# A linear-attention kernel: the store before the last is issued in five parts

## The chip, the cores and the metric

The kernel runs on one core of a Trainium2 chip. The metric is device time in microseconds (us) of one execution; smaller is better. Before the change three runs took 123.59 to 123.68 us, with a median of 123.68.

A core has five engines with instruction queues of their own: PE (matmul; its weight loads are listed as PEld), DVE (vector), ACT (scalar), POOL (general) and SP (which only synchronizes and issues transfers here). Transfers between the chip's main memory and the on-chip memory of 128 partitions are done by 16 DMA engines, and are issued from POOL, SP or ACT.

## The reference

Inputs Q, K and V are float32 of shape 8 x 12 x 512 x 64 (batch, heads, sequence, feature). For each of the 96 heads:

```
Q_feat = max(0, Q);  K_feat = max(0, K)
KV = K_feat^T V                      (64 x 64)
K_sum = sum of K_feat over the sequence
out = (Q_feat KV) / (Q_feat . K_sum + 1e-10)
```

The output has the shape of Q, in float32.

## The kernel before

The 96 heads are taken eight at a time, so there are NO = 12 groups, o = 0 to 11. One group of one tensor is 1 MB in main memory, seen as 128 partitions of 2048 float32, that is 8 KB in one run for each partition. A group of eight heads of output is such a block too.

Group 0 of K and V is loaded by SP and ACT as float32 into buffers that the output uses later (`k8`, `v8`). All other loads are issued by POOL (`load`, line 110), which converts to bf16 on the way: 4 KB a partition land in rings of six groups. The group's work runs through all engines: DVE masks and rectifies K and scales V (`prep`), PE transposes Q and multiplies K by V (`into`), ACT rectifies the transposed Q and copies KV, PE multiplies Q by KV and by K_sum, ACT copies the product (`ot`), PE transposes it back (`back`), and DVE multiplies it with the reciprocal of the denominator into one of eleven float32 buffers `o_sb` (`norm`, line 276). The groups overlap; group o's `norm` is done after group o+1's first half. At the end of its two halves, `norm` raises the semaphore NRM1.

Stores: `store(eng, o)` (lines 122 to 125) lets an engine wait for NRM1 and then issues one transfer of all 128 partitions from `o_sb` to the output. Groups 0 to 9 are stored from POOL, in POOL's queue between the loads and behind them. Groups 10 and 11 (NO - 2 and NO - 1) are stored from SP (lines 141 and 142), which has nothing else to do after its first load. POOL's transfers appear as queue q0 of the DMA engines, SP's as q1. Each completed transfer adds 16 to its semaphore: for the two stores of SP this is LAST.

SP ends the kernel: it waits for PE's last product (line 326), for the stores of POOL that no buffer's reuse waited for (ALL, line 327), and for LAST to reach 32 (line 328), and then clears the semaphores.

Of the kernel before, what the change touches and what calls it, by code (L numbers as in the profile page):

```python
# [5 lines left out]
def kernel(  # L6
# [9 lines left out]
    P = 128  # L16
# [4 lines left out]
    NO = B * H // 8  # L21
    assert NO * 8 == B * H and R == 16
    RING = 6
    NOUT = 11
# [7 lines left out]
    PE, PL, VE, AC, SP = nc.tensor, nc.gpsimd, nc.vector, nc.scalar, nc.sync  # L32

    def view(X):
        return X.rearrange("b h s d -> (b h s d)").rearrange("(n p f) -> n p f", p=P, f=RQ * D)

    Qr, Kr, Vr, Or = view(Q), view(K), view(V), view(out)

    def sb(name, shape, dt):
        return nc.alloc_sbuf_tensor(name, shape, dt)[:]  # L40
# [3 lines left out]
    def sems(*names):  # L44
        new = [nc.alloc_semaphore(n) for n in names]
        handles.extend(new)
        return new
# [9 lines left out]
    o_sb = [sb(f"o_sb{i}", [P, RQ, D], fp32) for i in range(NOUT)]  # L57
# [27 lines left out]
    ALL, LAST = sems("all", "last")  # L85
    stored = [sems(f"st{o}")[0] if o + NOUT < NO else ALL if o < NO - 2 else LAST for o in range(NO)]

    def land(name):
        landed[name], = sems(name)
        return landed[name]  # L90
# [4 lines left out]
    for eng, to, X, c in ((SP, k8, Kr, "k0"), (AC, v8, Vr, "v0")):  # L95
        d = eng.dma_start(out=to.rearrange("p r d -> p (r d)"), in_=X[0]).then_inc(land(c), 16)
# [22 lines left out]
        for i in range(o, o + n):  # L119
            run_of[i] = o  # L120

    def store(eng, o):
        eng.wait_ge(NRM1, o + 2)
        kw = {"single_packet": True} if eng is PL else {}
        eng.dma_start(out=Or[o], in_=o_sb[(o + 2) % NOUT].rearrange("p r d -> p (r d)"), **kw).then_inc(stored[o], 16)  # L125

    PL.memset(ident, 0.0).then_inc(ID, 1)
    PL.wait_ge(ID, 1)
# [2 lines left out]
    o, done = 1, 0  # L131
    for n in RUNS:
        while done < o + n - 1 - RING - HEAD + 1:
            store(PL, done)
            done += 1
        load(o, n)
        o += n
    assert o == NO
    for i in range(done, NO - 2):
        store(PL, i)  # L140
    for i in range(NO - 2, NO):
        store(SP, i)

    seen = set()

# [179 lines left out]

    SP.wait_ge(CO1, NO + 1)
    SP.wait_ge(ALL, 16 * (NOUT - 2))
    SP.wait_ge(LAST, 32)
    used = sorted(s.num for s in handles)
    assert used == list(range(used[0], used[-1] + 1))  # L330
    SP.sem_clear(range(used[0], used[-1] + 1))
# [28 lines left out]
```

## Time and profile before

The profile is of one execution of 123.92 us, of which the span from the first to the last instruction is 122.6 us.

| engine | busy us | share of the span |
|---|---|---|
| PE | 88.0 | 72% |
| DVE | 87.8 | 72% |
| ACT | 79.4 | 65% |
| POOL | 26.7 | 22% |

| transfers | issued | KB each on chip | median us from issue to landing |
|---|---|---|---|
| output, from POOL | 10 | 1024 | 39.0 |
| output, from SP | 2 | 1024 | 9.0 |
| Q, from POOL | 12 | 512 | 35.4 |
| K, from POOL | 11 | 512 | 32.1 |
| V, from POOL | 11 | 512 | 34.0 |

No compute engine is busy for more than 72% of the span. The long times from issue to landing are times in a queue: POOL issues well ahead of what the DMA engines can move. While loads run, the rate of the DMA engines in the profile counts the 4 KB that land of each 8 KB that are read, so 214 GB/s stand there where stores run at 425.

SP issues the store of group 10 at 106.79 us and that of group 11 at 113.45 us. The last store of POOL is issued at 98.44 us.

### The profile page before, as it was taken

The numbers are of one execution on the slowest core, as the hardware profiler recorded it, in microseconds if no ns is written. First come the engines' busy times: TensorE is split into PE (matmuls) and PEld (weight loads), VectorE is DVE, ScalarE is ACT, GpSimd is POOL, SyncE is SP. The second block draws the span as 40 slices with busy tenths as digits, with TensorE's granted clock in tenths as the row PEclk, the third lists the DMA queues.
The fourth block names the chain that finished last, engine by engine and source line by source line (L and its number), as shares of the span: only waits on it lengthen the run. The fifth ranks groups of instructions, "written<-read, shape, count | busy, mean of one in ns | idle before, by whom it ended". The sixth has DMA issues, their size and how long they took to land.

```text
span 122.6 us, 3398 instructions
## 1 busy us (share of the span) xinstructions
PE 88.0 (72%) x1480; PEld 75.4 (61%) x1480; DVE 87.8 (72%) x163; ACT 79.4 (65%) x109; POOL 26.7 (22%) x50
## 2 busy tenths in 40 slices
PE   0000069998998989989898998989899199768100
PEld 0000069986895958879596886958688189657100
DVE  1904924599999899999999999899993980927000
ACT  0043034999988888898889988888998285530000
POOL 2899700043050602409300101010010010000000
PEclk9999999999999999999999999999999959977855
DMA  3999999999999999999999999999999999999994
GB/s 80 401 317 214 214 210 212 212 212 214 214 214 214 214 214 214 215 214 214 214 214 212 214 214 212 214 212 341 255 214 298 428 425 428 425 428 425 425 430 182
DMA packets 6917, 32.56 MB, mean 266 GB/s; under 512 B 768, under 2 KB 768, under 8 KB 5120
## 3 DMA queue, kind: packets, MB, share of 16 engines
q0 software_dynamic: 6336, 28.31, 92.8%
q1 hardware_dynamic: 432, 3.15, 6.4%
q10 hardware_dynamic: 144, 1.05, 2.2%
q14 instruction: 4, 0.03, 0.1%
q8 instruction: 1, 0.02, 0.1%
HBM read 37.75 MB, written 12.58 MB: 410 GB/s over the span
## 4 chain that ended last, share of the span: by engine, by line
DMA 39%; PE 31%; DVE 19%; issue 1%; POOL 1%; ACT 1%; DVEq 0%
DMA q_all<-in_Q_dram 31%; DVE o_sb L276 13%; PE ps_kv L176 11%; PE ps_o L157 9%; DMA o_sb<-in_K_dram 8%; PE ps_q L169 6%; PE ps_o L197 4%; DVE kf L251 3%; DVE vo L257 2%; DVE q_sb L263 1%; ACT ot L237 1%; POOL v_all L117 1%; POOL k_all L117 0%; DVE den L287 0%; PE ps_q L189 0%
## 5 line engine op out<-in xcount | busy, mean ns | idle before, releaser
L276 DVE TENSOR_TENSOR o_sb<-ps_o,rec 128x1024 f32<-128x1024 f32 x24 | 28.4, 1220 | 8.5 <-PE ps_o L157 8.5
L237 ACT COPY ot<-ps_o 128x1024 f32<-128x1024 f32 x24 | 24.2, 1013 | 7.6 <-PE ps_o L197 6.2
L157 PE MATMUL ps_o<-ident,ot 128*128 128x128 f32 x208 | 27.2, 287 | 1.1 <-ACT ot L237 1.1
L176 PE MATMUL ps_kv<-vo,kf 64*128 64x132 bf16 x768 | 27.4, 225 | 0.0
L223 ACT ACTIVATE qt_sb<-ps_q 128x1024 bf16<-128x1024 bf16 x24 | 23.4, 1030 | 6.1 <-PE ps_q L169 6.1
L169 PE MATMUL ps_q<-ident,q_sb 128*128 128x128 bf16 x192 | 14.4, 235 | 16.3 <-DVE q_sb L263 16.3
L157 PEld LDWEIGHTS ps_o<-ident,ot 128*128 128x128 f32 x208 | 24.0, 147 | 2.7 <-ACT ot L237 1.4
L176 PEld LDWEIGHTS ps_kv<-vo,kf 64*128 64x128 bf16 x768 | 23.8, 97 | 2.9 <-issue 0.4
L169 PEld LDWEIGHTS ps_q<-ident,q_sb 128*128 128x128 bf16 x192 | 12.4, 106 | 18.7 <-DVE q_sb L263 16.3
L197 PE MATMUL ps_o<-qt_sb,kvd 128*128 128x256 bf16 x104 | 16.0, 279 | 8.7 <-DVE o_sb L276 8.3
L251 DVE TENSOR_SCALAR kf<-k_all,mask_k 128x1024 bf16<-128x1024 bf16 x44 | 18.4, 461 | 5.2 <-PE ps_kv L176 4.0
L228 ACT CAST kvd<-ps_kv 64x260 bf16<-64x260 f32 x48 | 18.0, 375 | 6.3 <-PE ps_kv L176 5.9
L197 PEld LDWEIGHTS ps_o<-qt_sb,kvd 128*128 128x128 bf16 x104 | 8.3, 99 | 13.8 <-DVE o_sb L276 12.0
L257 DVE TENSOR_SCALAR vo<-v_all,mask_v 128x1024 bf16<-128x1024 bf16 x33 | 14.9, 481 | 0.3 <-DMA v_all<-in_V_dram 0.3
L117 POOL DMA_DIRECT2D k_all<-in_K_dram x11 | 6.5, 592 | 32.7 <-DVE vo L257 32.5
L125 POOL DMA_DIRECT2D out_dram<-o_sb x10 | 5.3, 533 | 36.9 <-DVE o_sb L276 36.9
L217 ACT ACTIVATE vo<-v_all,mask_v 128x1024 bf16<-128x1024 bf16 x11 | 12.7, 1153 | 0.3
L263 DVE COPY q_sb<-q_all 128x2048 bf16<-128x2048 bf16 x12 | 8.3, 690 | 1.9 <-DMA q_all<-in_Q_dram 1.9
L117 POOL DMA_DIRECT2D v_all<-in_V_dram x11 | 7.8, 708 | 0.0
L189 PE MATMUL ps_q<-kvd,qt_sb 128*128 128x16 bf16 x208 | 7.5, 180 | 0.0
L189 PEld LDWEIGHTS ps_q<-kvd,qt_sb 128*128 128x128 bf16 x208 | 7.3, 96 | 0.3
L117 POOL DMA_DIRECT2D q_all<-in_Q_dram x11 | 6.7, 610 | 0.0
(21 smaller groups left out, 27.0 us busy)
## 6 DMA issues: line engine op xcount, KB each, us to landing
out_dram<-o_sb POOLq DMA_DIRECT2D x10, 1024.0 KB, 39.0
q_all<-in_Q_dram POOLq DMA_DIRECT2D x12, 512.0 KB, 35.4
k_all<-in_K_dram POOLq DMA_DIRECT2D x11, 512.0 KB, 32.1
v_all<-in_V_dram POOLq DMA_DIRECT2D x11, 512.0 KB, 34.0
out_dram<-o_sb SPq DMA_DIRECT2D x2, 1024.0 KB, 9.0
o_sb<-in_V_dram ACTq DMA_DIRECT2D x1, 1024.0 KB, 9.4
o_sb<-in_K_dram SPq DMA_DIRECT2D x1, 1024.0 KB, 9.6
```

Of the source, the lines that this page charges most:

```text
L117: PL.dma_start(out=t[:, to:to + n], in_=X[o:o + n].rearrange("n p f -> p n f"), single_packet=True).then_inc(land(f"{c}{o}"), 16)
L157: t = PE.transpose(ps_o[j][:, P * v:P * v + P], ot[:, 8 * j + v].rearrange("p h c -> p (h c)"), ident32)
L169: t = PE.transpose(dst[:, u], q_sb[:, j * (U // 2) + u], ident)
L176: t = PE.matmul(ps_kv[:, half, 0:2 * (D + 2)].rearrange("p (t d) -> p t d", t=2), kf[g][rows, r].rearrange("p s d -> p (s d)"), vo[g][rows ...
L189: t = PE.matmul(ps_den[:, u], qt_sb[:, u], kvd[:, :, 0:2 * D1:2 * D1 - 1], start=True, stop=True, skip_group_check=True)
L197: t = PE.matmul(ps[:, h], kvd[:, 4 * j + h, 1:2 * D + 1], q[:, :, 4 * j + h, :], start=True, stop=True, skip_group_check=True)
L223: AC.activation(qt_sb[:, j * (U // 2):(j + 1) * (U // 2)], ps_q[j].bitcast(bf16).rearrange("p (u f) -> p u f", u=U // 2), Act.Relu)
L228: t = AC.copy(kvd[64 * c:64 * c + 64, s::2, c * D1:c * D1 + D1].rearrange("p (g t) d -> p g t d", t=2), ps_kv[64 * s:64 * s + 64, :, 0:2 * ...
L237: t = AC.copy(ot[:, :, 4 * j:4 * j + 4], ps_o[j].rearrange("p (h u c) -> p u h c", h=4, u=U))
L251: VE.tensor_scalar(kf[g][:, :, s, :], k_rows(o, g), scalar1=0.0, scalar2=mask_k[:, s:s + 1], op0=Alu.max, op1=Alu.mult)
L257: x = VE.tensor_scalar(vo[g][:, :, t, 2:D + 2], v_rows(o, g), scalar1=mask_v[:, t:t + 1], scalar2=None, op0=Alu.mult)
L276: VE.tensor_tensor(dst[:, rs], ps_o[j].rearrange("p (r d) -> p r d", d=D), rec[o % 2][:, rs].unsqueeze(2).to_broadcast([P, R, D]), op=Alu. ...
```

## The change

The store of group 10 is issued as five transfers, of 112, 5, 5, 5 and 1 partitions in this order, one after the other from SP, behind one wait. The last store stays whole. As every part adds 16 to LAST, the wait at the end goes to 16 x 6 = 96.

```diff
-    def store(eng, o):
+    def store(eng, o, parts=(P,)):
         eng.wait_ge(NRM1, o + 2)
         kw = {"single_packet": True} if eng is PL else {}
-        eng.dma_start(out=Or[o], in_=o_sb[(o + 2) % NOUT].rearrange("p r d -> p (r d)"), **kw).then_inc(stored[o], 16)
+        to = 0
+        for n in parts:
+            eng.dma_start(out=Or[o, to:to + n], in_=o_sb[(o + 2) % NOUT][to:to + n].rearrange("p r d -> p (r d)"),
+                          **kw).then_inc(stored[o], 16)
+            to += n
+        assert to == P
...
-    for i in range(NO - 2, NO):
-        store(SP, i)
+
+    PARTS = (112, 5, 5, 5, 1)
+    store(SP, NO - 2, PARTS)
+    store(SP, NO - 1)
...
-    SP.wait_ge(LAST, 32)
+    SP.wait_ge(LAST, 16 * (len(PARTS) + 1))
```

## The prediction

> **What bounds the kernel now.** I read the page's slices first, then the chain that ended last, then SP's waits, then the last 16 us cut into short windows.
>
> The page's slices show which resource is full. The row "DMA" is the busy share of the 16 DMA engines in tenths, 3.07 us to a slice.
>
> ```profile
> DMA  3999999999999999999999999999999999999994
> GB/s 80 401 317 214 214 210 212 212 212 214 214 214 214 214 214 214 215 214 214 214 214 212 214 214 212 214 212 341 255 214 298 428 425 428 425 428 425 425 430 182
> ```
>
> The engines stand at nine tenths or more from the second slice to the last but one, while the page's rows of all compute engines show 0 in the last two. The end is set by the DMA engines emptying their queues. In the chain that ended last, the compute part stops long before the span's end of 122.6:
>
> ```profile
> 112.20 1.24 DVE o_sb L276
> 113.44 0.05 issue
> 113.48 0.61 PE ps_o L197 x4
> ```
>
> The chain follows instructions and so runs out at 114.1; the 8.5 us behind it are transfers. SP's waits say so:
>
> ```profile
> SPq L125 <- DVE o_sb L276: 111.2, 2, 104.9
> SPq L328 <- DMA out_dram<-o_sb: 8.6, 1, 8.6
> ```
>
> SP waits 8.6 us at line 328 for the two stores that it issued itself. The wait ends at 122.4, and nothing but the clearing of the semaphores follows.
>
> The windows of the tail (columns: window, its length, busy us of PE, PEld, DVE, ACT and POOL, PE's granted clock, DMA share, GB/s) show how the 16 engines stop:
>
> ```profile
> 113.50:119.60 6.10, 0.59 (x4) 0.29 (x4) 0.00 (x0) 0.00 (x0) 0.00 (x0) 0.66 1.02 430
> ...
> 120.20:120.50 0.30, 0.00 (x0) 0.00 (x0) 0.00 (x0) 0.00 (x0) 0.00 (x0) 0.50 0.90 382
> 120.50:120.80 0.30, 0.00 (x0) 0.00 (x0) 0.00 (x0) 0.00 (x0) 0.00 (x0) 0.50 0.59 246
> 120.80:121.10 0.30, 0.00 (x0) 0.00 (x0) 0.00 (x0) 0.00 (x0) 0.00 (x0) 0.50 0.40 164
> 121.10:121.40 0.30, 0.00 (x0) 0.00 (x0) 0.00 (x0) 0.00 (x0) 0.00 (x0) 0.50 0.20 82
> 121.40:121.70 0.30, 0.00 (x0) 0.00 (x0) 0.00 (x0) 0.00 (x0) 0.00 (x0) 0.50 0.13 55
> 121.70:122.00 0.30, 0.00 (x0) 0.00 (x0) 0.00 (x0) 0.00 (x0) 0.00 (x0) 0.50 0.01 0
> ```
>
> From the first line comes the price of a row (one partition of a store, 8 KB): 430 GB/s over 16 engines is 26.9 GB/s each, and 8192 bytes at that are 0.305 us. The others are a staircase. GB/s by 0.30 us by one row of 8192 bytes gives the rows begun in each window: 14, 9, 6, 3, 2 and none. As a row lasts as long as a window, these are engines still at work. Ten of the 16 begin nothing after 120.8; three begin something after 121.1, two after 121.4. The two last end near 121.8 (share 0.01 of 16 engines for 0.30 us is 0.05 us), and the wait ends 0.6 us later. If all engines stopped together, the six late ones' 6 + 3 + 2 = 11 rows would be shared by 16, so about 0.7 row or 0.2 us after 120.9 instead of 0.9. Some 0.7 us of unevenness is there; the page doesn't number the engines, so which ones are late it doesn't say.
>
> **The change part by part.** *Rows moved.* Parts of 112, 5, 5, 5 and 1 partitions, if they land on the engines as the change's own words have it, give every engine 7 rows, the first five three or (four of them) two more: 10 or 11 where all had 8. Against before, the first engine gets +3 rows (+0.915 us), the next four +2 (+0.61), the other eleven -1 (-0.305); 3 + 8 = 11, nothing is lost. Every engine is busy from the issue at 106.79 to its own end (shares of 1.01 and 1.02 from 106.8 to 119.6), so a row moved shifts the engine's end by the whole row.
>
> If the late engines are among the eleven, their end goes from 121.8 to 121.5. The first five then come from the ten that begin nothing after 120.8. These end between about 120.5 and 121.1, the middle at 120.8, and with their rows four end at 121.1 to 121.7 and the first at 121.4 to 122.0. The new last end lies between 121.5 and 122.0, a change of -0.3 to +0.2. I take -0.28, near the full row: rows begun fall from 14 to 9 between 120.2 and 120.8, and of those 9 six belong to engines that go on, so most of the ten are done by 120.8; besides, the wait ends 0.6 us after the last row, which leaves the first five some margin if their completion is quicker than the two last engines'.
>
> [...]
>
> *Issues.* Four more on SP. The two of before took 332 and 343 ns (SP's issues on line 125), so 4 x 0.338 = 1.35 us. They follow the wait for NRM1 that ends at 106.79, so the fifth is out by 108.5. Behind them in SP's queue stands the last store, which waits for DVE until 113.45. Cover 6.66 us, needed 1.7: nothing. Without the cover it would cost 1.35 us. No other engine waits for SP, and the q1 queue still has rows of the 112 by then (a store of 8 rows an engine took 9.0 us from issue to landing), so the late issue starves no engine. Bounds 0 and +1.35; I take 0.
>
> *Completions.* Each transfer brings 16 small packets (48 issues, 768 packets under 512 B on the page), and their time lies inside the 430 GB/s above. The parts of 5, 5, 5 and 1 bring four more to the first engine and three to the next four. Bounds: nothing, and a row's time for each, 1.22 on the first engine; by the 430 GB/s, which already hold such packets, I take 0.
>
> *The semaphore.* LAST counts to 96 where it counted to 32: one wait as before, behind which nothing stands. Zero.
>
> *Reading by sevens.* A store of 112 rows isn't cut over the engines as one of 128 is. An engine's seven rows may lie in partitions that another engine reads at that moment for POOL's stores. No row shows a transfer of another cut. Bounds by rows: 0, or each of seven rows taking the time of two and as many of the engine's other rows held up by strangers: 14 x 0.305 = 4.3 us. Rows of all 48 transfers keep one rate; I take 0, and the upper end makes a rival.
>
> Sum: 123.92 for the profiled execution (span 122.6 and 1.3 around it), less 0.28: 123.64. It stands 0.24 above the runs' median of 123.68, so for the median I predict 123.40.
>
> **Rivals.** *Engines in one another's way* (slower). Place: the seven rows of each engine, from 108 to 113, beside POOL's stores in the other queue. If partitions share a way out of the memory that carries about one engine's 26.9 GB/s, two engines on one way take 0.61 us for a row. One doubled row on a late engine eats the gain, a second makes it slower. Half the bound above, 2.1, less 0.3, gives 125.5; the whole 127.7. For it: the engines have no slack (shares of 1.0 to 119.6), so each stall reaches the end; the parts of five read neighbouring partitions at once. Against it: two queues feed the engines from 108.8 on, and a stalled row might be overlapped by the next. I hold it next in likelihood to the forecast.
>
> [...]
>
> *A late engine among the first five.* 121.8 + 0.61 or + 0.915, so +0.6 to +0.9: 124.3 to 124.6. It is the two engines that begin rows after 121.4 that decide: a third, ending near 121.5, would come to 122.1 with two more rows, neither gain nor much loss. Drawn blindly, both of the two are among the eleven with 11 x 10 / (16 x 15) = 0.46. Nothing on the page numbers them, so the profile speaks neither for nor against beyond that draw; I go above it for the forecast, since two engines that stand apart from the rest of the staircase are likelier a trait of certain engines than a draw, and there are more numbers from the sixth up.
>
> [...]
>
> *The parts don't go where they should.* If small parts spread over all engines, each keeps 8 rows: 123.68 with nothing gained, 123.9 with some small packets.
>
> **How the numbers follow.** A measurement of this kernel can tell about 0.2% (0.25 us). The forecast has 0.42, of which 0.35 over 0.2% faster and 0.07 within it, since -0.28 lies next to the border; engines in one another's way 0.32, all slower; a late engine among the five 0.21, slower; the parts elsewhere 0.05, of which 0.03 within and 0.02 slower. Faster 0.35, same 0.07 + 0.03 = 0.10, slower 0.32 + 0.21 + 0.02 = 0.55. The likeliest case's own range is 123.25 to 123.65. The range for 8 in 10 runs from 123.1 to 126.4: beyond it lie somewhat under half of engines in one another's way (0.14) and a little below.
>
> **What would show it.** Right: SP has six issues of stores, five of them from 106.8 to 108.5; the compute lines to 114.1 are unmoved; the tail's windows keep 430 GB/s up to 119.6, the staircase is steeper and SP's wait at 328 is some 0.3 us shorter. Engines in one another's way: the GB/s between 109 and 118 fall below 420 with the DMA share still at 1. A late one among the five: full rate, but one or a few engines still begin rows after 121.9. The forecast is wrong if the wait at 328 ends at 122.4 or later.

## The result, and the profile after

The changed kernel takes 124.47 us (median of 4 runs, 124.28 to 124.53) against 123.68 of before (now four runs, 123.59 to 124.01). The ratio is 1.0056, 95% interval 1.0035 to 1.0078: 0.8 us slower, where 0.28 us less was forecast. A second measurement of the same kernel (below) gave 1.0090, interval 1.0059 to 1.0122. The profiled execution took 124.53 us with a span of 123.2, against 123.92 and 122.6.

The page's slices of after, the same two rows as shown of before:

```profile
DMA  4999999999999999999999999999999999999992
GB/s 88 404 309 215 214 211 213 214 213 213 213 213 213 215 213 214 214 213 214 211 214 215 214 214 213 217 211 376 222 214 339 428 428 420 426 426 420 410 426 109
```

The loads' part is the same up to the small changes of any two executions. The DMA engines are full to the last slice but one again. The chain that ended last stops where it did (114.0 against 114.1), so the compute part did not move:

```profile
112.12 1.24 DVE o_sb L283
113.40 0.61 PE ps_o L204 x4
```

SP's waits, with the final one now at line 335:

```profile
SPq L127 <- DVE o_sb L283: 109.1, 2, 104.9
SPq L335 <- DMA out_dram<-o_sb: 9.3, 1, 9.3
```

It is 9.3 us where it was 8.6, and ends at 122.8 (plus 0.18 of its own) instead of 122.4. The windows of the tail (window, length, busy us of PE, PEld, DVE, ACT and POOL, PE's clock, DMA share, GB/s):

```profile
113.50:119.60 6.10, 0.51 (x4) 0.21 (x3) 0.00 (x0) 0.00 (x0) 0.00 (x0) 0.64 1.02 419
120.20:120.50 0.30, 0.00 (x0) 0.00 (x0) 0.00 (x0) 0.00 (x0) 0.00 (x0) 0.50 0.59 246
120.50:120.80 0.30, 0.00 (x0) 0.00 (x0) 0.00 (x0) 0.00 (x0) 0.00 (x0) 0.50 0.33 137
120.80:121.10 0.30, 0.00 (x0) 0.00 (x0) 0.00 (x0) 0.00 (x0) 0.00 (x0) 0.50 0.39 164
121.10:121.40 0.30, 0.00 (x0) 0.00 (x0) 0.00 (x0) 0.00 (x0) 0.00 (x0) 0.50 0.39 164
121.40:121.70 0.30, 0.00 (x0) 0.00 (x0) 0.00 (x0) 0.00 (x0) 0.00 (x0) 0.50 0.26 109
121.70:122.00 0.30, 0.00 (x0) 0.00 (x0) 0.00 (x0) 0.00 (x0) 0.00 (x0) 0.50 0.26 109
122.00:122.30 0.30, 0.00 (x0) 0.00 (x0) 0.00 (x0) 0.00 (x0) 0.00 (x0) 0.50 0.20 82
122.30:122.70 0.40, 0.00 (x0) 0.00 (x0) 0.00 (x0) 0.00 (x0) 0.00 (x0) 0.50 0.01 0
```

Two things differ from before. The rate from 113.5 to 119.6 is 419 GB/s, not 430, with the share at 1.02 as it was: the engines are busy all the time and move less. And the staircase is longer. By GB/s times 0.30 us over 8192 bytes the rows begun are 9, 5, 6, 6, 4, 4, 3, 0, where before they were 14, 9, 6, 3, 2, 0 in the windows from 120.2 on. Most engines stop earlier than before, which is the row less that they have; but six engines begin a row in each of the windows from 120.8 to 121.4, which fits five engines with added rows and one other late one (the table below bears this out). Three begin a row after 122.0, where before nothing began after 121.7.

### The profile page after: what moved, and what is told of

The parts are those of the page before. It is cut to its first block, busy times and chain, and to the rows that moved or that the text cites. A ratio compares the mean times of both kernels' runs of the same rounds, so it can differ in the third digit from the quotient of the medians.

```text
span 123.2 us, 3402 instructions
## 1 busy us (share of the span) xinstructions
PE 87.8 (71%) x1480; PEld 75.2 (61%) x1480; DVE 87.8 (71%) x163; ACT 79.4 (64%) x109; POOL 26.7 (22%) x50
## 4 chain that ended last, share of the span: by engine, by line
DMA 39%; PE 30%; DVE 19%; issue 1%; POOL 1%; ACT 1%; DVEq 0%
DMA q_all<-in_Q_dram 31%; DVE o_sb L283 12%; PE ps_kv L183 11%; PE ps_o L164 9%; DMA o_sb<-in_K_dram 8%; PE ps_q L176 6%; PE ps_o L204 4%; DVE kf L258 3%; DVE vo L264 2%; DVE q_sb L270 1%; ACT ot L244 1%; POOL v_all L117 1%; POOL k_all L117 0%; DVE den L294 0%; PE ps_q L196 0%
```

## The experiments

Two theories were set against each other after this result. L: late engines are among the first five, and their extra rows make the end. W, later sharpened to N: the way in which the store is cut costs; N says that rows which several engines read at once from neighbouring partitions last longer. The first five are the engines that the change's parts of five use, and the first is the one of them that the part of one uses: in the change's trace the same five of 16 chains of packets (below) have one row of each part of five, and one of the five chains has a fourth small row. That parts of other sizes take these engines in one and the same order is the author's assumption. All runs were timed beside runs of the kernel before on the same chip. The ratio is an estimate of its own, not the quotient of the two medians; where the two give different microseconds, the text says which is meant.

| run | what SP issues in place of the whole store of group 10 | median us | before beside it | ratio, 95% interval |
|---|---|---|---|---|
| e1 | 112, 16 | 124.05 | 123.79 | 1.0021 (1.0002 to 1.0041) |
| e2 | whole, and two loads of 5 neighbouring partitions | 124.62 | 123.79 | 1.0057 (1.0036 to 1.0077) |
| e3 | whole, and two loads of 1 partition | 123.72 | 123.79 | 0.9994 (0.9980 to 1.0009) |
| e4 | 112, 8, 8 | 124.27 | 123.79 | 1.0045 (1.0022 to 1.0068) |
| e5 | 112, four times 4, neighbours | 125.11 | 123.76 | 1.0095 (1.0066 to 1.0125) |
| e6 | 112, four times 4, every fourth partition | 124.42 | 123.76 | 1.0057 (1.0040 to 1.0074) |
| e7 | whole, and two loads of 5 spread partitions | 124.36 | 123.76 | 1.0037 (1.0021 to 1.0053) |
| e8 | 112, 15, 1 | 124.30 | 123.76 | 1.0028 (1.0009 to 1.0048) |
| e9 | 112, 5, 5, 5, 1, the fives in steps of three | 124.41 | 124.02 | 1.0046 (1.0032 to 1.0060) |
| e10 | the change again: 112, 5, 5, 5, 1 | 124.97 | 124.02 | 1.0090 (1.0059 to 1.0122) |
| e11 | whole, and two loads of 2 spread partitions | 123.93 | 124.02 | 1.0004 (0.9984 to 1.0024) |
| e12 | whole, and two loads of 4 spread partitions | 124.13 | 124.02 | 1.0015 (1.0003 to 1.0027) |

### Rows added to the first engines, nothing else changed

e2 and e3 keep before's store whole and add transfers behind it that only cost time. The loads fill a part of `k_all` that nothing reads any more; n is 5 or 1:

```diff
+    for x in range(2):
+        SP.dma_start(out=k_all[0:n, 2 * x:2 * x + 2].rearrange("p n r d -> p (n r d)").bitcast(fp32),
+                     in_=Kr[0, 0:n]).then_inc(LAST, 16)
```

> Before's whole store, and behind it two loads of 5 partitions of 8 KB each into a part of k_all that is no longer read: added work of two rows for each of the first five engines, none taken away. Theory L: the first five hold the last engine or one close to it, so the end moves by most of two rows, +0.4 to +0.6: 124.1 to 124.3. If the first five were among those that end at 120.5 to 121.1, the end moves by 0 to +0.1: 123.7 to 123.8. Theory W gives the latter too.

> As the run with loads of 5 partitions, with loads of 1 partition: two rows for the first engine alone. Theory L with the first engine itself late: +0.4 to +0.6, 124.1 to 124.3; with the late ones second to fifth: 123.7 to 123.8. Theory T: each added transfer costs whatever its rows, +0.2 to +0.3 here and in the run with 5.

Two rows more on the first engine alone change nothing (0.9994). Two on each of the first five make it 0.7 us longer. The windows of the tail of e3, then of e2:

```profile
121.10:121.40 0.30, 0.00 (x0) 0.00 (x0) 0.00 (x0) 0.00 (x0) 0.00 (x0) 0.50 0.20 82
121.40:121.70 0.30, 0.00 (x0) 0.00 (x0) 0.00 (x0) 0.00 (x0) 0.00 (x0) 0.50 0.01 0
```

```profile
121.10:121.40 0.30, 0.00 (x0) 0.00 (x0) 0.00 (x0) 0.00 (x0) 0.00 (x0) 0.50 0.33 137
121.40:121.70 0.30, 0.00 (x0) 0.00 (x0) 0.00 (x0) 0.00 (x0) 0.00 (x0) 0.50 0.26 109
121.70:122.00 0.30, 0.00 (x0) 0.00 (x0) 0.00 (x0) 0.00 (x0) 0.00 (x0) 0.50 0.20 82
122.00:122.30 0.30, 0.00 (x0) 0.00 (x0) 0.00 (x0) 0.00 (x0) 0.00 (x0) 0.50 0.07 27
```

With the added rows on one engine the last row begins before 121.4 (three engines in 121.1 to 121.4, then none), no later than in before. With five engines it begins after 122.0. Both runs add two transfers, so transfers as such (theory T in the expectations) cost nothing that can be seen. The first engine has room for two rows; somewhere among the second to fifth is one that has none. That is theory L. The measured 0.7 us (by the ratio, interval 0.45 to 0.95) is a little more than the two rows' 0.61.

### Which of the first five

e7, e11 and e12 do the same with loads of 5, 2 and 4 rows that go to partitions 25 apart:

```diff
-        SP.dma_start(out=k_all[0:n, 2 * x:2 * x + 2].rearrange("p n r d -> p (n r d)").bitcast(fp32),
-                     in_=Kr[0, 0:n]).then_inc(LAST, 16)
+        SP.dma_start(out=k_all[0:25 * n:25, 2 * x:2 * x + 2].rearrange("p n r d -> p (n r d)").bitcast(fp32),
+                     in_=Kr[0, 0:25 * n:25]).then_inc(LAST, 16)
```

> Before's whole store and two loads of 5 partitions behind it, as in the earlier run, but to partitions 0, 25, 50, 75 and 100 instead of 0 to 4. Two rows more for the first five engines. Theory L+N: +0.2 to +0.4, 124.0 to 124.2, less than the +0.7 with neighbouring partitions. Theory L alone: +0.6 to +0.8 again.

> Before's whole store and two loads of 2 partitions (0 and 25): two rows more for the first two engines. If the late one of the first five is the second: +0.3 to +0.5, 124.1 to 124.3, like the spread loads of 5. If it is among the third to fifth: 123.7 to 123.9.

> Before's whole store and two loads of 4 partitions (0, 25, 50, 75): two rows more for the first four engines. Late one among the second to fourth: 124.1 to 124.3. If it is the fifth alone: 123.7 to 123.9.

Two engines: nothing (1.0004). Four: 0.19 us by the ratio (0.0015 of 124.02), interval just clear of none. Five: 0.46 us by the ratio. So the second engine has room like the first, the third or fourth is somewhat late, and the fifth more. The times in the expectations were counted from a before of 123.8, and before stood at 124.02 beside e11 and e12, so the differences count: one late engine among the second to fourth was to give +0.3 to +0.5, the fifth alone nothing. The 0.19 lies between, and more than one late engine fits better.

The packets themselves tell which engines are late. An engine's packets follow one another without a gap (in these traces the next begins 3 ns before the end of the last), so the packets of a trace sort into 16 chains. The number of 8 KB rows that a chain has between two completions of SP's queue shows whether its engine took part in a small transfer. The last packet of a chain ends at, in us:

| run | engines with added rows | the latest of the others |
|---|---|---|
| before | none | 121.86 |
| e3 | 121.15 | 121.63 |
| e11 | 121.23, 121.58 | 121.91 |
| e12 (this execution took 124.55, the longest of its runs) | 121.07, 121.37, 121.69, 122.69 | 122.43 |
| e7 | 120.94, 121.26, 121.50, 122.19, 122.40 | 121.74 |
| the change | 121.92, 122.22, 122.33, 122.35, 122.50 | 121.57 |
| e9 (below) | 121.29, 121.32, 121.40, 122.04, 122.39 | 121.68 |

In e3 and e11 the engines with two rows more still end before another. In e7 two of the five make the end. One of these is the fifth engine. From about 98 to 115 us one engine's rows last 0.31 to 0.39 us instead of 0.309 (in before some 45 rows, 1.0 us more in sum), and in the traces with parts of five (the change, e7, e9, e10) one row of the first such part is one of these (0.313 to 0.327), while with parts of four (e6, e12) none is. This engine ends at 121.75 in before, at 122.35 in the change and at 122.40 in e7. The other, 122.19 in e7 and 122.33 in the change, can only be the third or the fourth, if it is the same one in every trace. That it and an engine outside the first five end late has nothing to do with long rows: by 100 us their chains already stand two to four rows behind most others.

That five spread rows cost 0.46 us and five neighbouring ones 0.70 pointed to N, but the intervals overlap. In e2's trace it is not the added rows that are long (0.31 us) but five rows of POOL's stores right behind them (0.43 to 0.71). The next runs test N on stores.

### The cut by sevens, and even parts

```diff
-    PARTS = (112, 5, 5, 5, 1)
+    PARTS = (112, 16)          # e1; e4: (112, 8, 8)
```

> The store before the last in parts of 112 and 16 partitions. If the parts land as the change's words have it, every engine has its 8 rows again. Theory L (the five engines that got more rows hold the late ones; their extra rows alone made the time longer): 123.7, as before, within 0.15. Theory W (the way the store is cut costs: rows by sevens in one another's way): most of the 0.8 us stays, 124.2 to 124.5, and the rate between 106.8 and 119.6 is about 420 GB/s rather than 430. Theory T (more transfers cost, each some 0.15 us): 123.8 to 123.9.

> Parts of 112, 8 and 8: one more row for the first eight engines, one less for the other eight. Theory L: +0.2 to +0.3, 123.9 to 124.0, since the late ones among the first five have one row more. Theory W: like the run with 112 and 16, 124.2 to 124.5. If late engines were mostly from the ninth up: 123.4.

e1 gives every engine its eight rows again and is 0.26 us slower than before, between what L (nothing) and W (most of 0.8) gave. e4 gives one row more to each of the first eight engines: 0.56 us by the ratio, nearly twice what a row costs and, with 124.27, within what W gave, so not L's rows alone either. Something in the cut costs, and it is not the 112. Between 109 and 112 us, when its rows and POOL's are under way together, after moves as much as before (packets and rate in the window, and SP's queue; first after, then before):

```profile
DMA packets 172, 1.28 MB, mean 426 GB/s; under 512 B 16, under 2 KB 16, under 8 KB 16
q1 hardware_dynamic: 55, 0.45, 35.4%
```

```profile
DMA packets 167, 1.26 MB, mean 421 GB/s; under 512 B 13, under 2 KB 13, under 8 KB 13
q1 hardware_dynamic: 52, 0.43, 33.5%
```

426 GB/s by sevens against 421 by eights: the rows of the large part as a whole are not in one another's way, though single ones are long (one of 0.50 us in the change at 112.6, a few of 0.5 to 0.8 in e1, e8 and e10). The cost must lie mostly in the small parts.

### Small parts of neighbours, and of partitions apart

e5 and e6 put the same rows on the same engines, three more on each of the first four. They differ only in which of the last 16 partitions make up a part: 112 to 115, then 116 to 119 and so on in e5; 112, 116, 120, 124, then 113, 117 and so on in e6.

```diff
-        to = 0
-        for n in parts:
-            eng.dma_start(out=Or[o, to:to + n], in_=o_sb[(o + 2) % NOUT][to:to + n].rearrange("p r d -> p (r d)"),
+        for x, n in enumerate(parts):
+            rows = slice(0, n) if n >= 112 else slice(111 + x, P, 4)
+            eng.dma_start(out=Or[o, rows], in_=o_sb[(o + 2) % NOUT][rows].rearrange("p r d -> p (r d)"),
...
-    PARTS = (112, 5, 5, 5, 1)
+    PARTS = (112, 4, 4, 4, 4)          # e5 and e6; the lines above in e6 alone
```

> Parts of 112, 4, 4, 4 and 4 partitions, each small part of neighbouring partitions: the first four engines get three more rows than before, the others one less. Theory L+N (rows on late engines count, and rows that several engines read at once from neighbouring partitions last longer): at least +0.9 for a late engine among the four, less its distance from the last: 124.4 to 125.2, and in the windows between 114.5 and 117 a rate below 410 GB/s. Theory L alone: 124.3 to 124.6, with 430 GB/s there.

> The same rows on the same engines as the run with 112, 4, 4, 4 and 4, but each small part takes every fourth of the last 16 partitions (112, 116, 120, 124 and so on), so that no part reads neighbours at once. Theory N: 0.3 to 0.6 us shorter than with neighbouring rows, and no window between 114.5 and 117 below 420 GB/s. Theory L alone: the same time as with neighbouring rows, within 0.15.

Neighbours cost 1.0095, partitions four apart 1.0057. By the medians 0.69 us lie between them, a little over the 0.3 to 0.6 that N gave, by the ratios 0.47; the two intervals just overlap. The row's own time shows why. The DMA queues in a short window where rows of a first small part begin (packets, MB, and their time as a share of 16 engines over the window), e5 from 113.1 to 113.5, then e6 from 114.6 to 115.1:

```profile
q0 software_dynamic: 23, 0.15, 87.8%
q1 hardware_dynamic: 11, 0.03, 53.0%
```

```profile
q0 software_dynamic: 28, 0.20, 97.0%
q1 hardware_dynamic: 6, 0.03, 15.7%
```

The small packets are completions of 9 ns, so the time belongs to the 8 KB rows: 0.03 MB are four. In e5, 53.0% of 16 engines for 0.4 us is 3.39 us, or 0.85 us a row on average. In e6, 15.7% of 16 for 0.5 us is 1.26 us, or 0.31 us a row, the ordinary time. In the change itself, from 114.7 to 115.1, and in before from 114.5 to 115.2:

```profile
q0 software_dynamic: 18, 0.15, 86.9%
q1 hardware_dynamic: 9, 0.04, 57.6%
```

```profile
q0 software_dynamic: 28, 0.23, 77.2%
q1 hardware_dynamic: 20, 0.07, 25.8%
```

After: 0.04 MB, five rows (one to each of the first five engines), in 57.6% of 16 x 0.4 = 3.7 us, 0.74 us each on average. Before: nine rows in 25.8% of 16 x 0.7 = 2.9 us, 0.32 each. Row by row, after's five are of 0.46, 0.73, 1.01 and 1.14 us on the first four engines, and of 0.32 on the fifth; if the engines take the rows in their order, which the trace doesn't show, the four are partitions 112 to 115 and the fifth is 116. e5 has five rows between 0.59 and 1.13; e6 has none over 0.40, where an ordinary row is 0.309. It is the same in the other cuts with neighbours: all eight rows of e4's first small part took 0.42 to 1.44 us, five of e8's fifteen 0.45 to 1.76, four of e1's sixteen 0.56 to 0.87. Mainly the first small part is hit: in after the rows of the second begin between 115.87 and 116.68, no longer within the time of one row. In the rate it shows as well, after first, then before:

```profile
114.50:115.50 1.00, 0.00 (x0) 0.00 (x0) 0.00 (x0) 0.00 (x0) 0.00 (x0) 0.87 1.01 369
```

```profile
114.50:115.50 1.00, 0.00 (x0) 0.00 (x0) 0.00 (x0) 0.00 (x0) 0.00 (x0) 0.96 1.03 434
```

e5's windows between 114.5 and 117 did not fall below 410 GB/s as N expected. The loss came earlier, 377 GB/s from 113.5 to 114.5; e6 has 451 there. And e6 has 393 from 115.5 to 116.5, below the 420 that N gave: rates of one window also swing in before (410 there), so the time of a row is the better reading.

### The change with its small parts apart

e9 is the change with the same rows on each engine, the fives taken from 112 to 126 in steps of three; e10 is the change again.

```diff
...
+            rows = slice(0, n) if n >= 112 else slice(111 + x, 124 + x, 3) if n == 5 else slice(127, P)
...
```

Otherwise e9's `store` is that of e6.

> The change with other rows in its small parts: 112, then partitions 112, 115, 118, 121, 124, then 113 to 125 and 114 to 126 in the same steps, then 127. Rows by engine are those of the change, but few of a part are neighbours. Theory L+N (a late engine among the first five gets two rows, and neighbouring rows read at once last longer): between the two, 124.0 to 124.3, 0.2 to 0.4 below the change run beside it, and no window of 1 us after 114 that falls to 370 GB/s. Theory L alone: the time of the change, within 0.15. Theory N alone: 123.4 to 123.7.

> The change itself, beside the run with other rows, for their difference: 124.4 to 124.6, 0.56% above before as first measured.

The change was slower than expected (1.0090), and e9 1.0046, 0.56 us less by the medians beside each other and outside each other's interval but for a sliver (1.0060 and 1.0059). Against the change's first measurement, 1.0056, e9 saves only 0.1. Neighbours in the small parts thus cost 0.1 to 0.6 us of the change; what the late engines' rows cost, 0.0046 of 124.02 = 0.57 us, stays. The two profiles of the change show such a spread: in the first the last engine ends 0.15 us after the fifth (122.50 against 122.35), in e10 0.64 us after it (123.07 against 122.42), each with a row of over 1.1 us in its first small part. The tail of e9:

```profile
120.80:121.10 0.30, 0.00 (x0) 0.00 (x0) 0.00 (x0) 0.00 (x0) 0.00 (x0) 0.50 0.40 164
121.10:121.40 0.30, 0.00 (x0) 0.00 (x0) 0.00 (x0) 0.00 (x0) 0.00 (x0) 0.50 0.20 82
121.40:121.70 0.30, 0.00 (x0) 0.00 (x0) 0.00 (x0) 0.00 (x0) 0.00 (x0) 0.50 0.13 55
121.70:122.00 0.30, 0.00 (x0) 0.00 (x0) 0.00 (x0) 0.00 (x0) 0.00 (x0) 0.50 0.13 55
122.00:122.30 0.30, 0.00 (x0) 0.00 (x0) 0.00 (x0) 0.00 (x0) 0.00 (x0) 0.50 0.07 27
122.30:122.70 0.40, 0.00 (x0) 0.00 (x0) 0.00 (x0) 0.00 (x0) 0.00 (x0) 0.50 0.00 0
```

The rows begun are 6, 3, 2, 2, 1, 0: a single engine makes the end after 122.0, the fifth, where the change has three.

### A miss: a row less for the last engine

e8 takes a row from the sixteenth engine only:

```diff
-    PARTS = (112, 5, 5, 5, 1)
+    PARTS = (112, 15, 1)
```

> Parts of 112, 15 and 1: 9 rows for the first engine, 8 for the next fourteen as before, 7 for the last. If the very last engine to end is the sixteenth, its row less takes up to 0.3 us off the end and the 15 neighbouring rows give about 0.26 back, as with 112 and 16: 123.7 to 123.8. If it isn't: like 112 and 16, 123.9 to 124.1.

1.0028, like e1 (1.0021) or worse: either the sixteenth is not the engine that ends last in before, or the 15 neighbours read at once hide it. The trace says the first: the one chain without a row of the 15 ends at 120.36, early even with a row more, and the last one ends at 122.93. The neighbours cost beside it: the engine that ends last, the one with the slightly long rows, has a row of 1.55 us.

## Why the prediction failed

**What bounds the kernel** held: full DMA engines to the end, an unmoved compute part, and the end set by engines that run out one by one. By the prediction's own signs the forecast fell (the wait ends at 122.8, not before 122.4), and those of both rivals came: 419 GB/s at a full share, and rows begun after 121.9.

**Rows moved.** The step that failed is "If the late engines are among the eleven". The fifth engine and the third or fourth are late themselves. They got two rows more, 0.61 us, of which e7 shows 0.46 and e9 0.57 at the end. The fifth went from 121.75 to 122.35, as the sum with two rows more has it. The row less of the others was worth nothing, since the end was no longer theirs: the latest of them ends at 121.57, where before ended at 121.86. The forecast's sum holds for that engine, if it is the one that ended last before. This was the rival of a late engine among the first five. Its price of +0.6 to +0.9 is close to e9's 0.57; the change's 0.8 has the delay of the neighbouring rows in it. Its chance of 0.21 was set too low: the staircase counted late engines but did not number them, the blind draw of 0.46 for the two last was raised to twice the rival's chance without a row to do so, and the third late engine was waved aside. The prediction's "Rows of all 48 transfers keep one rate" also passed over the one engine whose rows are longer, which already was in before's trace. e7 (1.0037) and e11 (1.0004) together place late engines between the third and the fifth, and the sixteenth, without a row of e8's 15, ends early there, at 120.36.

**Which engines a part uses** held as the change has it, though no run had shown it when the forecast was made. From 106 us on SP's queue has 48 completion packets in the change's trace, which is 16 + 5 + 5 + 5 + 1 + 16, where before's has 32; 11 of the 16 chains have seven rows of the part of 112 and eight of the last store, the five others a row of each part of five besides. The runs fit an order from the first engine on, with two rows more changing nothing for one and two partitions (e3, 0.9994; e11, 1.0004) and the end for five (e7, 1.0037), and with the engine of the long rows (0.313 to 0.327 us) in the first part of five and in none of the parts of four (e6, e12). Early completions came for the four small parts at 107.7 to 109.3, ahead of any of their rows.

**Reading by sevens**, taken at nothing, was right for the part of 112: 426 GB/s against 421. The rival of engines in one another's way had the wrong place, the seven rows, but its second argument, "the parts of five read neighbouring partitions at once", names what cost time: 0.83 us on average instead of 0.31 for four of the five rows of the first such part in the change. Its price of +1.8 was too high by a factor of three or more, since it counted half of 14 rows of an engine where one to two are hit. That partitions share a way out of the memory was the author's supposition, and no run shows what makes the rows long. The four long rows took 1.35 us from the first start to the last end in the change and 1.19 in e5, near the 1.22 us of four rows of 0.305 us one after the other; but single rows of 1.44 us in e4 and of 1.76 in e8 are longer than that. The fifth row beside the four took 0.32 us in the change, and rows four partitions apart (e6) none over 0.40.

**Issues** were underestimated without effect. The five took 106.78 to 109.11, 2.3 us instead of 1.7, single ones 0.27 to 0.65 us; the last store's wait until 113.4 covered them.

**Completions** at nothing was right (e3: two more on one engine, 0.9994). **The semaphore** was right.

**A version that beats before** was not found. An engine that carries fewer rows than the ones above it cannot be had from parts that all begin at the first engine, as the change's four small ones do (that engine's chain has a row of each), and it is engines from the third to the fifth that would need fewer (e7, e11). The fifth's longer rows add up to 1.0 us, about what it is late by (121.75, where ten engines end at 120.3 to 121.0). Why these rows are longer, and why the other late ones stand behind by 100 us, was not tried and stays open.

## What to carry to other kernels

A tail that drains unevenly can be evened only if one knows which engines are late; find it by adding a transfer of one, two or more partitions at the end and seeing from which size the time moves, before moving work to them. When a transfer is split into small parts, take their partitions apart from one another, here by steps of four: the rows of four neighbouring partitions read at once took 0.85 us on average in e5, those of partitions four apart 0.31 in e6.

## What was not expected of the hardware

A transfer of 112 partitions ran beside 128-partition ones at their rate (426 GB/s against before's 421), so in this place a cut by sevens did not cost the rate. Neighbouring rows read by several engines at once took up to 1.14 us in the change and up to 1.76 in e8, rows three or four partitions apart at most 0.41. And in every trace one of the 16 engines, the fifth wherever the parts show its number, has rows of 0.31 to 0.39 us instead of 0.309 from about 98 to 115 us.
